# The last group's attention by row tiles, and form steps placed anew, in a two-layer hybrid decoder trunk

## The chip, the cores and the metric

The kernel runs on one core of a Trainium2 chip. The core has a matrix engine (TensorE, here PE, whose weight loads are shown apart as PEld), a vector engine (VectorE, DVE), a scalar engine (ScalarE, ACT), GpSimd (POOL) and a queue engine (SyncE, SP) that issues transfers; POOL issues transfers too. Each engine works through its own instructions in the order in which they were written and stops at one whose inputs are not ready. The metric is the device time of one execution in microseconds (us), lower is better.

## The reference

`x` has 256 rows and 2048 columns, all in float32. Two layers of this, and a last RMSNorm:

```python
h = rms_norm(x, norm_g)
p = split_columns(einsum("bsd,de->bse", h, w_in))     # fox, diff, moba, gla: q, k, v, g each
fox  = forgetting_attention(...)        * silu(p["fox_g"])
diff = rms_norm(differential_attention(...)) * silu(p["diff_g"])
moba = moba_attention(...)              * silu(p["moba_g"])   # 256 rows: one causal block
gla  = rms_norm(gla_chunked(...))       * silu(p["gla_g"])
mixed = concatenate([fox, diff, moba, gla], axis=-1)  # 4 groups of 512 columns, 4 heads each
x = x + einsum("bse,ed->bsd", mixed, w_out)
```

In `moba_attention` 256 rows are one key block, so it is causal softmax attention `softmax(q k^T / sqrt(128)) v` for four heads. With two row tiles of 128 rows, row tile 0 attends to keys 0 to 127 alone, row tile 1 to both halves of the keys.

## The kernel before

**Weights.** Every weight step loads 128x1024 numbers (a `raw` tile; `RAW_BUFS` of them) and splits them into two parts of reduced precision, `hi` (ACT) and `lo` (DVE, `raw` minus `hi`); four pairs of part tiles exist (`PART_BUFS`). The activations are split in the same way: `hTh`/`hTl` for the input projection (`hTp` in the rows), `mTh`/`mTl` for the output projection. PE then makes three products, hi x hi, hi x lo and lo x hi, for each k tile and both row tiles: 12 matmuls of 128x512 for a step. Some projections are formed in pairs from sums and differences of two weight matrices ("form steps", in the rows those with `raw<-xs,raw` or `xs<-xs,raw` on DVE); the table `FORMS_AT` says after which projection step of a layer each of them stands.

**Order.** The program is written out by a planner in Python. The list of PE's weight steps (`plan`) is fixed; between its matmuls, `fill` lets helper tasks (the four groups' attention) put in their instructions when a cost model says that their inputs are ready (`passive` for PE and the queues, `choose` for ACT and DVE). `STALL`, `LOADED`, `ISSUE` and the like are constants of this model. What comes out is one fixed order for each engine. All recorded operations carry the line of the helper, L481 (in the changed kernel L482).

**The end of a layer.** The output projection has four blocks of 512 columns: c0, c1, c2 and chunk 3. The groups are multiplied in the order gla, fox, diff and last moba (`OUT_ORDER`), two steps for each group and block. `moba`'s `attend` makes the scores, the softmax and a transposition; the transposed weights go out to memory (`far<-four`, SP) and come back (`four<-far`, POOL) for each row tile. Then 12 P·V matmuls of 128x128 (4 for row tile 0, 8 for row tile 1) write a PSUM tile `side<-four,four`, DVE multiplies by the gate (`four<-side,four`), and `split_group` makes `mTh` on ACT and `mTl` on DVE, in two halves by heads (`PIECES`). `attend` waits for the transposed weights of both row tiles before its first P·V matmul. The first output block's last two steps need the halves ("m", l, 4) and ("m", l, 5); c2's steps for the third group (`side<-hi,mTh` and the like) stand right before them on PE.

**Gated linear attention.** For each of two pairs of heads DVE makes factors for 7 levels. In the wide way (`GLA_WIDE`), 7 multiplications write one tile of 128 partitions (`four<-eight,four`), and two ACT copies spread it over the zero-padded tile `tq`; in the other way 14 multiplications of 64 partitions write `tq` at once (`tq<-eight,four`). Layer 0 uses the wide way, layer 1 the other. `tq` is a weight of PE's `side<-tq,eight`.

## Time and profile before

| | |
|---|---|
| median of 3 runs | 884.09 us (883.62 to 884.95) |
| the profiled execution | 883.46 us |
| its span, first to last instruction | 881.7 us |
| busy: PE, PEld | 865.9 us (98%), 734.0 us (83%) |
| busy: DVE, ACT, POOL | 763.5 us (87%), 600.7 us (68%), 61.1 us (7%) |
| TensorE's granted clock, mean | 0.998 of full speed |
| moved by DMA | 235.99 MB, 268 GB/s on average |

The profiled execution's time is the span and 1.8 us around it. Busy shares are averages over the span; where one engine waits for another is read from the waits and the timeline of the stretch in question. A wait is put down to the producer that came last by the profile.

### The profile page before, as it was taken

How to read it: one execution, taken by the hardware profiler on the slowest of the kernel's cores; microseconds unless marked ns; L12 is line 12 of the kernel's file. 1: busy time of each engine (PE TensorE's matmuls, PEld its weight loads, DVE VectorE, ACT ScalarE, POOL GpSimd, SP SyncE). 2: the span in 40 equal slices, each digit the busy share in tenths (PEclk: the TensorE clock that was granted, in tenths of full speed). 3: DMA queues.
4: the chain of work that ended last, by engine and by line, in shares of the span. 5: the costliest groups of instructions: out<-in, count | busy, mean ns of one | idle time of the engine just before them, and what ended most of it. 6: DMA issues, size and time to landing. Idle time of an engine off the chain costs nothing.

```text
span 881.7 us, 12530 instructions
## 1 busy us (share of the span) xinstructions
PE 865.9 (98%) x4276; PEld 734.0 (83%) x4276; DVE 763.5 (87%) x993; ACT 600.7 (68%) x945; POOL 61.1 (7%) x82
## 2 busy tenths in 40 slices
PE   9999999999999999999999999999999999999996
PEld 7998788798878888887899888888888788888786
DVE  5779999999999989766768799999999999987583
ACT  7778966756787586754756985576577776777351
POOL 1000100011001001000000010001110100010000
PEclk9999999999999999999999999999999999999999
DMA  8978958799799968995888896699898999789832
GB/s 299 301 277 290 270 196 262 251 258 319 275 303 293 310 236 259 336 324 191 248 282 299 284 246 245 191 307 259 249 332 286 280 307 310 227 264 338 287 118 96
DMA packets 86264, 235.99 MB, mean 268 GB/s; under 512 B 9768, under 2 KB 30136, under 8 KB 86072
## 3 DMA queue, kind: packets, MB, share of 16 engines
q1 hardware_dynamic: 76936, 202.41, 68.2%
q0 software_dynamic: 8832, 31.99, 14.2%
q10 hardware_dynamic: 432, 0.80, 0.2%
q8 instruction: 33, 0.54, 0.2%
q14 instruction: 31, 0.25, 0.1%
HBM read 212.61 MB, written 22.55 MB: 267 GB/s over the span
## 4 chain that ended last, share of the span: by engine, by line
PE 90%; DVE 3%; DMA 2%; issue 1%; ACT 1%; SPq 0%; POOLq 0%; POOL 0%; DVEq 0%; ACTq 0%
PE mm L481 76%; PE side L481 15%; DVE lo L481 2%; DMA four<-far 1%; DMA xs<-in_weights 1%; DMA raw<-in_weights 1%; DVE four L481 1%; DVE tq L481 0%; DVE raw L481 0%; ACT hi L481 0%; DMA far<-four 0%; DVE eight L481 0%; ACT four L481 0%; DVE xs L481 0%; ACT eight L481 0%
## 5 line engine op out<-in xcount | busy, mean ns | idle before, releaser
L481 ACT ACTIVATE hi<-raw 128x1024 fp32r<-128x1024 f32 (+2 forms) x319 | 317.4, 1009 | 151.3 <-PE mm L481 76.5
L481 DVE TENSOR_TENSOR lo<-raw,hi 128x1024 fp32r<-128x1024 f32 (+2 forms) x319 | 362.8, 1156 | 53.4 <-ACT hi L481 46.0
L481 PE MATMUL mm<-hi,hTp 128*128 128x512 f32 (+1 forms) x1440 | 353.5, 379 | 1.1 <-ACT hTp L481 0.4
L481 PEld LDWEIGHTS mm<-hi,hTp 128*128 128x128 f32 x1440 | 262.7, 188 | 50.8 <-issue 1.9
L481 PE MATMUL mm<-lo,hTp 128*128 128x512 f32 (+1 forms) x720 | 196.4, 378 | 0.2 <-DVE lo L481 0.2
L481 PEld LDWEIGHTS mm<-lo,hTp 128*128 128x128 f32 x720 | 131.8, 188 | 25.5 <-DVE lo L481 2.1
L481 PE MATMUL mm<-hi,mTh 128*128 128x512 f32 (+1 forms) x384 | 110.4, 385 | 5.4 <-ACT mTh L481 3.0
L481 PE MATMUL mm<-lo,mTh 128*128 128x512 f32 (+1 forms) x384 | 108.7, 381 | 0.7 <-DVE lo L481 0.7
L481 PE MATMUL mm<-hi,mTl 128*128 128x512 f32 (+1 forms) x384 | 108.6, 381 | 0.0
L481 ACT ACTIVATE hi<-xs 128x1024 fp32r<-128x1024 f32 x72 | 76.0, 1061 | 25.2 <-PE mm L481 24.1
L481 DVE TENSOR_TENSOR lo<-xs,hi 128x1024 fp32r<-128x1024 f32 x72 | 86.0, 1217 | 0.9 <-ACT hi L481 0.8
L481 PEld LDWEIGHTS mm<-hi,mTh 128*128 128x128 f32 x384 | 69.0, 188 | 18.6 <-ACT mTh L481 3.4
L481 PEld LDWEIGHTS mm<-lo,mTh 128*128 128x128 f32 x384 | 70.1, 188 | 15.5 <-DVE lo L481 1.8
L481 PEld LDWEIGHTS mm<-hi,mTl 128*128 128x128 f32 x384 | 70.3, 188 | 14.1
L481 DVE TENSOR_TENSOR xs<-xs,raw 128x1024 f32<-128x1024 f32 x48 | 58.4, 1218 | 0.0
L481 POOL DMA_DIRECT2D four<-far x40 | 21.9, 548 | 505.0 <-DVE lo L481 113.9
L481 PEld LDWEIGHTS side<-four,four 128*128 128x128 f32 (+1 forms) x328 | 38.5, 190 | 4.4 <-issue 2.1
L481 PE MATMUL side<-four,four 128*128 128x128 f32 (+3 forms) x328 | 42.0, 293 | 0.1
L481 DVE STREAM_TRANSPOSE four<-four 128x1024 f32<-128x1024 f32 (+1 forms) x34 | 38.3, 1141 | 0.8 <-ACT four L481 0.7
L481 ACT ACTIVATE four<-mm,rstd 128x512 f32<-128x512 f32 (+2 forms) x44 | 28.0, 663 | 15.8 <-PE mm L481 15.4
L481 ACT ACTIVATE four<-side 128x128 f32<-128x128 f32 (+3 forms) x66 | 15.9, 264 | 23.9 <-PE side L481 23.3
L481 ACT ACTIVATE four<-four 128x1024 f32<-128x1024 f32 (+3 forms) x28 | 25.6, 928 | 9.2 <-DMA four<-far 7.8
(142 smaller groups left out, 727.7 us busy)
## 6 DMA issues: line engine op xcount, KB each, us to landing
raw<-in_weights SPq DMA_DIRECT2D x271, 512.0 KB, 5.2
four<-far POOLq DMA_DIRECT2D x34, 512.0 KB, 6.4
far<-four SPq DMA_DIRECT2D x128, 128.0 KB, 3.9
raw<-in_weights SPq DMA_DIRECT2D x46, 348.0 KB, 5.0
xs<-in_weights SPq DMA_DIRECT2D x24, 512.0 KB, 6.0
xs<-in_weights POOLq DMA_DIRECT2D x24, 512.0 KB, 9.2
xs<-in_x SPq DMA_DIRECT2D x4, 512.0 KB, 6.7
kept<-xs SPq DMA_DIRECT2D x1, 2048.0 KB
```

What stands on the lines that cost most here:

```text
L481: op.do()
```

## The change

The last group's attention (moba) of each layer no longer goes through the common end of `attend`: `last_products` takes row tile 0's transposed weights as soon as they are there, makes its 4 P·V matmuls, its gate, `mTh` and `mTl`, and then does the same for row tile 1, whose 8 P·V matmuls may be written up to 1.5 us of model time ahead of their inputs (`safe`). The first output block's two last steps are multiplied by row tiles (`multiply_rows`): first row tile 0 with both steps (12 matmuls), then row tile 1 (12). Beside that, `GLA_WIDE` is set for layer 1 too, there is one raw tile more, three constants of the planner's model are others, and of `FORMS_AT` about a quarter of the entries move by one to four steps. The rows of `MIDDLE` change too, but the projections among them that are steps of their own keep their order in both layers. The number of PE's matmuls is the same.

```diff
-RAW_BUFS = 6
+RAW_BUFS = 7
...
-FORMS_AT = ((26, 29, 31, 32, 33, 33, 33, 34, 35, 35, 35, 35, 36, 36, 37, 37, 38, 38, 39, 39, 40, 40, 40, 41, 43,
+FORMS_AT = ((26, 29, 31, 32, 33, 33, 33, 34, 35, 35, 35, 35, 36, 36, 36, 37, 38, 38, 38, 39, 40, 41, 41, 41, 43,
...
-STALL = 0.3
+STALL = 0.1
...
-LOADED = 6.0
+LOADED = 5.0
...
-ISSUE = 0.45
+ISSUE = 0.6
...
-PIECES = 2
+LAST_STEPS = 0
+LAST_SAFE = -1.5
 GLA_ABS = (True, False)
-GLA_WIDE = (True, False)
+GLA_WIDE = (True, True)
...
-                    if not (op.kind == "do" or op.kind == "t" and due + SAFE <= times.now
+                    if not (op.kind == "do" or op.kind == "t" and due + (SAFE if op.safe is None else op.safe) <= times.now
...
             t0, p0 = yield from joined(boxes[0])
+            if gi == OUT_ORDER[l][-1]:
+                yield from last_products(l, gi, vn, sg, t0, p0, boxes[1], sgt)
+                return
             t1, p1 = yield from joined(boxes[1])
...
+    def last_products(l, gi, vn, sg, t0, p0, box, sgt):
...
+        for h in range(H):
+            matmul(o[:, 0, h], vh[h][0], p0[:, h], True, True)
+        s2.put(t0)
+        yield
+        every = slice(0, H)
+        gate(0, every)
+        yield
+        low = high(0, every)
+        yield
+        low()
+        given_out(("m0", l))
+        t1, p1 = yield from joined(box)
+        for _ in range(LAST_STEPS):
+            yield
+        for h in range(H):
+            matmul(o[:, 1, h], vh[h][0], p1[:, 2 * h], True, False, safe=LAST_SAFE)
+            matmul(o[:, 1, h], vh[h][1], p1[:, 2 * h + 1], False, True, safe=LAST_SAFE)
+        s4.put(t1, vn)
+
+        def results_out():
+            halves = [slice(0, H // 2), slice(H // 2, H)]
+            for hs in halves:
+                gate(1, hs)
+            lows = [high(1, hs) for hs in halves]
...
+            for i, f in enumerate(lows):
+                f()
+                given_out(("m", l, 2 * gi + i))
...
+    def multiply_rows(s, m):
+        b = s["block"]
+        lh, ll = b["lhs"]
+        order = list(enumerate(s["kts"]))
+        products = [(x, part, j, kt) for x, part in ((lh, "hi"), (lh, "lo"), (ll, "hi")) for j, kt in order]
+        for k, (x, part, j, kt) in enumerate(products):
+            matmul(b["ps"][m][:, :b["n"]], x[:, kt, m * P:(m + 1) * P], s[part][:, j], False, s["last"] and k == len(products) - 1, main=True)
...
-        prepare(i + ahead)
+        prepare(i + ahead - (i - 1 in by_rows_at))
...
-            multiply(s)
+            if i in by_rows_at:
+                multiply_rows(s, 0)
+            elif i - 1 in by_rows_at:
+                multiply_rows(s, 0)
+                for z in (plan[i - 1], s):
...
+                    times.now = max([times.now] + [ready[k] for k in z["later"]])
+                    multiply_rows(z, 1)
+            else:
+                multiply(s)
```

**PE, end of layer 0.** In the kernel before, this is the end of block c2 (`side_3516`), the P·V matmuls (`side_3721`, of which one stands further up among the products of c2, not shown) and the start of the first output block (`mm_3261` is row tile 0, `mm_3262` row tile 1):

```order
L481 MATMUL side_3516<-hi,mTl 128x512 x4
L481 MATMUL side_3516<-lo,mTh 128x512 x4
L481 MATMUL side_3721<-four_3629,four_1659 128x128 x2
L481 MATMUL side_3721<-four_3462,four_1659 128x128
L481 MATMUL side_3721<-four_3629,four_1659 128x128 x2
L481 MATMUL side_3721<-four_3462,four_1659 128x128
L481 MATMUL side_3721<-four_3629,four_1659 128x128 x2
L481 MATMUL side_3721<-four_3462,four_1659 128x128
L481 MATMUL side_3721<-four_3629,four_1659 128x128 x2
L481 MATMUL mm_3261<-hi,mTh 128x512
L481 MATMUL mm_3262<-hi,mTh 128x512
L481 MATMUL mm_3261<-hi,mTh 128x512
```

In the changed kernel (c2 is `side_3518`, P·V `side_3633`, the first output block's row tile 0 `mm_3263`):

```order
L482 MATMUL side_3518<-hi,mTh 128x512 x4
L482 MATMUL side_3518<-hi,mTl 128x512 x2
L482 MATMUL side_3633<-four_3632,four_1741 128x128 x8
L482 MATMUL side_3518<-hi,mTl 128x512 x2
L482 MATMUL side_3518<-lo,mTh 128x512 x4
L482 MATMUL mm_3263<-hi,mTh 128x512 x2
L482 MATMUL mm_3263<-lo,mTh 128x512 x2
L482 MATMUL mm_3263<-hi,mTl 128x512 x2
L482 MATMUL mm_3263<-hi,mTh 128x512 x2
L482 MATMUL mm_3263<-lo,mTh 128x512 x2
L482 MATMUL mm_3263<-hi,mTl 128x512 x2
L482 MATMUL mm_3264<-hi,mTh 128x512 x2
```

Row tile 1's 8 P·V matmuls now stand 6 matmuls ahead of c2's end, and 12 products of row tile 0 follow before `mm_3264`, row tile 1, begins; row tile 0's 4 P·V matmuls stand 30 matmuls ahead of these 8. Layer 1's end has the same pattern.

**DVE, layer 0, gated linear attention at about 120 us.** `four1_1081<-mm2_753` takes a projection's results from PSUM, `lo_...` are weight parts, `raw<-xs,raw` sums of a form step, `eight0_997` the factors. Before:

```order
L481 SCALAR_TENSOR_TENSOR four1_1081<-mm2_753,r-1.0_606,four1_1081 128x512
L481 TENSOR_TENSOR eight0_997<-eight0_997,four11_876 128x2x4x16
L481 TENSOR_TENSOR lo_1229<-raw_1110,hi_1228 128x1024
L481 TENSOR_TENSOR lo_1240<-raw_1122,hi_1239 128x1024
L481 TENSOR_TENSOR eight0_997<-eight0_997,four11_876 128x2x8x8
L481 TENSOR_TENSOR lo_1261<-raw_1135,hi_1260 128x1024
L481 TENSOR_TENSOR raw_1159<-xs_83,raw_1159 128x1024
L481 TENSOR_TENSOR raw_1206<-xs_83,raw_1206 128x1024
L481 TENSOR_TENSOR eight0_997<-eight0_997,four11_876 128x2x16x4
```

After, from the same place:

```order
L482 SCALAR_TENSOR_TENSOR four1_1083<-mm2_755,r-1.0_608,four1_1083 128x512
L482 TENSOR_TENSOR eight0_999<-eight0_999,four11_878 128x2x4x16
L482 TENSOR_TENSOR lo_1222<-raw_1101,hi_1221 128x1024
L482 TENSOR_TENSOR lo_1242<-raw_1112,hi_1241 128x1024
L482 TENSOR_TENSOR raw_1124<-xs_83,raw_1124 128x1024
L482 TENSOR_TENSOR raw_1161<-xs_83,raw_1161 128x1024
L482 TENSOR_TENSOR eight0_999<-eight0_999,four11_878 128x2x8x8
L482 TENSOR_TENSOR eight0_999<-eight0_999,four11_878 128x2x16x4
L482 TENSOR_TENSOR lo_1263<-raw_1124,hi_1262 128x1024
```

The two sums and one `eight` operation now stand ahead of the third `lo` (`lo_1263`), which belongs to a form step; before, the third `lo` (`lo_1261`, of a projection step) stood ahead of the sums. On PE, `lo_1263` is used four matmuls after the place where before the projection step of `lo_1261` began; `lo_1261` was used eight matmuls after that place.

**POOL, layer 1, from the reads for gla's second pair to the end of the forgetting attention's keys.** `four5_5816` (before) and `four11_5735` (after) hold transposed keys for the forgetting attention's scores; `rsh` is a reciprocal root for gla's norm:

```order
L481 DMA four0_5315<-far0_5436 128x1024
L1823 DMA xs_83<-in_weights 128x1024 x4
L481 TENSOR_TENSOR rsh_5893<-pw_5892,halfpow_88 128x8
L481 DMA four5_5816<-far1_5826 128x1024
L481 DMA four11_5817<-far2_5829 128x1024
L481 DMA four3_5828<-far3_5883 128x1024
```

After:

```order
L482 DMA four12_5320<-far0_5419 128x1024
L1885 DMA xs_83<-in_weights 128x1024 x4
L482 DMA four11_5735<-far1_5738 128x1024
L482 TENSOR_TENSOR rsh_5860<-pw_5859,halfpow_88 128x8
L482 DMA four7_5785<-far2_5793 128x1024
L482 DMA four10_5786<-far3_5812 128x1024
```

The read of these keys has moved ahead of `rsh`. On ACT the copy that waits for this read has moved too, from behind the three `hi` of the steps ahead of the scores to a place ahead of three `hi`; on PE the scores stand 24 matmuls earlier.

## Rows read from the trace of the kernel before

**Rows 1.** The page's busy time of each engine: microseconds, share of the span, number of instructions.

```profile
PE 865.9 (98%) x4276; PEld 734.0 (83%) x4276; DVE 763.5 (87%) x993; ACT 600.7 (68%) x945; POOL 61.1 (7%) x82
```

**Rows 2.** PE's waits over the whole span: what waited, for which engine's tile, microseconds in total, times, the longest.

```profile
PE mm L481 <- ACT mTh L481: 3.0, 2, 1.5
PE mm L481 <- ACT eight L481: 1.6, 1, 1.6
PE mm L481 <- DVE lo L481: 0.9, 2, 0.7
PE mm L481 <- ACT four L481: 0.8, 1, 0.8
...
PE mm L481 <- DVE four L481: 0.2, 1, 0.2
```

**Rows 3.** Busy time by stretch: the stretch and its length, then for PE, PEld (weight loads), DVE, ACT and POOL the busy time (and instructions), the granted clock, the share of the DMA engines, GB/s.

```profile
112.00:250.00 138.00, 137.83 (x691) 116.51 (x690) 135.13 (x183) 94.77 (x150) 7.88 (x10) 1.00 0.82 263
...
530.00:660.00 130.00, 128.18 (x639) 109.21 (x638) 126.77 (x192) 82.40 (x129) 8.76 (x10) 1.00 0.82 262
```

**Rows 4.** Timeline, end of layer 0: start, duration, engine, operation, what it writes and reads, number of like records, and in brackets idle time before it and what ended it. Each 128x128 f32 matmul leaves two records.

```profile
394.87 1.09 PE L481 MATMUL side<-hi,mTh 128*128 128x512 f32 x4
...
395.80 1.07 PE L481 MATMUL side<-hi,mTl 128*128 128x512 f32 x4
...
397.54 2.53 PEld L481 LDWEIGHTS side<-four,four 128*128 128x128 f32 x22 [0.20 <-DMA four<-far]
397.61 2.65 PE L481 MATMUL side<-four,four 128*128 128x128 f32 x22
...
400.30 1.42 DVE L481 TENSOR_TENSOR four<-side,four 128x256 f32<-128x256 f32 x4 [1.08 <-PE side L481]
...
401.78 1.20 PE L481 MATMUL mm<-hi,mTh 128*128 128x512 f32 x4 [1.51 <-ACT mTh L481]
```

**Rows 5.** Timeline of POOL, end of layer 0: the reads of the two row tiles of the last group's transposed weights are issued.

```profile
382.43 0.55 POOL L481 DMA_DIRECT2D four<-far  x1 [13.88 <-DVE lo L481]
389.85 0.53 POOL L481 DMA_DIRECT2D four<-far  x1 [6.87 <-DMA far<-four]
```

**Rows 6.** DMA issues of two stretches, 383 to 398 us (first row) and 815 to 830 us (the others): queue, number, KB each, microseconds from issue to landing.

```profile
four<-far POOLq DMA_DIRECT2D x1, 512.0 KB, 7.7
...
four<-far POOLq DMA_DIRECT2D x1, 512.0 KB, 5.7
four<-far POOLq DMA_DIRECT2D x1, 256.0 KB, 4.0
```

**Rows 7.** Timeline, end of layer 1: POOL's issue of the read of row tile 1, and PE's weight loads for the P·V products.

```profile
822.16 0.53 POOL L481 DMA_DIRECT2D four<-far  x1 [5.82 <-DMA far<-four]
...
830.23 2.65 PEld L481 LDWEIGHTS side<-four,four 128*128 128x128 f32 x22
```

**Rows 8.** Timeline, layer 1, around the first run of `tq` multiplications.

```profile
537.19 4.19 DVE L481 TENSOR_TENSOR tq<-eight,four 64x128 f32<-64x128 f32 x14
...
545.40 2.01 ACT L481 ACTIVATE hi<-raw 128x1024 fp32r<-128x1024 f32 x2 [6.61 <-DVE raw L481]
...
553.51 0.73 PE L481 MATMUL mm<-lo,mTh 128*128 128x512 f32 x2 [0.72 <-DVE lo L481]
```

**Rows 9.** Timeline, layer 1, five records from 621 to 649 us: behind the second run of `tq` multiplications, and at the scores of the forgetting attention.

```profile
621.49 0.75 DVE L481 SCALAR_TENSOR_TENSOR four<-mm,rstd,four 128x512 f32<-128x512 f32 x1
...
622.39 0.70 PE L481 MATMUL mm<-hi,mTh 128*128 128x512 f32 x2 [0.78 <-ACT four L481]
...
636.88 2.57 POOL L481 TENSOR_TENSOR rsh<-pw,halfpow 128x8 f32<-128x8 f32 x1 [20.68 <-DVE pw L481]
...
647.45 1.06 ACT L481 ACTIVATE four<-four 128x1024 f32<-128x1024 f32 x1 [3.23 <-DMA four<-far]
...
648.56 1.62 PEld L481 LDWEIGHTS side<-four,four 128*128 128x128 f32 x12 [0.39 <-ACT four L481]
```

**Rows 10.** The same step of the gated linear attention in layer 0, where it is done the wide way: DVE's timeline (first two), and ACT's group of copies in the whole kernel (number, busy time, mean ns of one, idle time before them).

```profile
110.04 0.69 DVE L481 TENSOR_TENSOR four<-eight,four 128x128 f32<-128x128 f32 x3
...
111.78 0.89 DVE L481 TENSOR_TENSOR four<-eight,four 128x128 f32<-128x128 f32 x4
...
L481 ACT ACTIVATE tq<-four 64x896 f32<-64x896 f32 x4 | 3.8, 949 | 0.4 <-DVE four L481 0.3
```

**Rows 11.** Timeline, layer 0, around 125 us: DVE (first three) and PE.

```profile
119.98 2.35 DVE L481 TENSOR_TENSOR lo<-raw,hi 128x1024 fp32r<-128x1024 f32 x2
...
123.59 2.36 DVE L481 TENSOR_TENSOR raw<-xs,raw 128x1024 f32<-128x1024 f32 x2
125.86 0.90 DVE L481 TENSOR_TENSOR eight<-eight,four 128x128 f32<-128x128 f32 x4
...
124.36 1.98 PE L481 MATMUL mm<-hi,hTp 128*128 128x512 f32 x8
...
128.14 0.73 PE L481 MATMUL mm<-lo,mTh 128*128 128x512 f32 x2
```

**Rows 12.** The page's costliest groups (two rows: number, busy time, mean ns of one, idle time just before them and what ended most of it) and its DMA issues (last row).

```profile
L481 ACT ACTIVATE hi<-raw 128x1024 fp32r<-128x1024 f32 (+2 forms) x319 | 317.4, 1009 | 151.3 <-PE mm L481 76.5
...
L481 POOL DMA_DIRECT2D four<-far x40 | 21.9, 548 | 505.0 <-DVE lo L481 113.9
...
xs<-in_weights POOLq DMA_DIRECT2D x24, 512.0 KB, 9.2
```

More of the change, by code (lines that the diff above doesn't have):

```diff
@@ L580, in until, with matmul @@
             cur["task"].latest = max(cur["task"].latest, ready[key])
-    def matmul(out, lhsT, rhs, start, stop, tiles=1, main=False, **kw):
+    def matmul(out, lhsT, rhs, start, stop, tiles=1, main=False, safe=None, **kw):
         n = int(np.prod(rhs.shape[1:]))
@@ L1192, in attend @@
         vn, (sgt, sg) = env[name + "_v", l], env[name + "_g", l]
-        split = name in SPLIT_P
+        split = name in SPLIT_P and gi != OUT_ORDER[l][-1]
         if split:
@@ L1219, in attend @@
             yield
+        mixed = yield from s4.take([P, 2 * H, P])
         ops = yield from take_side()
@@ L1243, in attend @@
         yield
-        mixed = yield from s4.take([P, 2 * H, P])
-        pieces = PIECES if gi == OUT_ORDER[l][-1] else 1
-        for i in range(pieces):
-            hs = slice(i * H // pieces, (i + 1) * H // pieces)
-            for m in range(2):
-                at = slice(m * H + hs.start, m * H + hs.stop)
-                v_.tensor_mul(in_squares(mixed.rearrange("p (h m) t -> p m h t", m=2)[:, m, hs]), in_squares(o[:, hs, m]), sg[:, at])
-            if i == pieces - 1:
-                side.put(ops)
-                s4.put(sgt)
-            begin(split_group(l, gi, mixed, "h m", hs), l, gi)
@@ L1585, in hybrid_trunk @@
         plan.append({**z, "block": b, "need": {(b["need"], b["l"], k // (4 if b["need"] == "h" else 2)) for k in z["kts"]}})
+    by_rows_at = set()
+    for i, s in enumerate(plan[:-1]):
+        z = s.get("block")
+        if z and s["kts"][0] // 4 == OUT_ORDER[z["l"]][-1] and z["need"] == "m" and z is blocks[z["l"] * LAYER + LAYER - 4] and not s["last"]:
+            assert plan[i + 1].get("block") is z and plan[i + 1]["last"]
+            by_rows_at.add(i)
+            for t in plan[i:i + 2]:
+                t["later"], t["need"] = t["need"], {("m0", z["l"])}
     xts = []
@@ L2133, in hybrid_trunk @@
                     b["banks"], b["ps"] = zip(*[take_bank() for _ in range(2)])
-            multiply(s)
+            if i in by_rows_at:
[3 more added lines that the diff above has]
+                for z in (plan[i - 1], s):
+                    loads["left"] = lasts(s)
+                    fill()
+                    while not z["later"] <= ready.keys():
+                        tick(False)
+                    times.now = max([times.now] + [ready[k] for k in z["later"]])
+                    multiply_rows(z, 1)
+            else:
+                multiply(s)
             if s["last"] and b["done"]:
```

36 lines of the change are left out of this document (30 added, 6 removed).

## The prediction, made before the changed kernel ran

> **What bounds the kernel now.** I read the busy shares first: PE is busy 98% of the span and DVE 87% [rows 1]. So a gain can only come out of the little time in which PE stands still, and that is the second view, PE's waits: 6.5 us in the five kinds shown [rows 2], the rest, under 2 us, at the very start. The reader is to see there which waits the change can reach. The largest, 3.0 us for ACT's `mTh`, is two waits of 1.5 us, one at the end of each layer. The 1.6 us for ACT's `eight` falls at 100 us, where the order of all engines is the same in both kernels, so it stays. DVE `lo`, ACT `four` and DVE `four` add 1.9 us. The third view, busy time by stretch, tells what stands behind the smaller waits: in 112 to 250 us DVE works 135.13 of 138 us, in 530 to 660 us 126.77 of 130 [rows 3]. In these two stretches, where each layer's gated linear attention runs, DVE is nearly as full as PE, and one more DVE microsecond in front of a weight part is paid by PE. The last view is the timeline around each of the named waits.
>
> **Last group, layer 0.** PE's last c2 products lead to 11 P·V matmuls (22 records, 397.61 to 400.26); then DVE gates (400.30), ACT makes `mTh`, and PE goes on at 401.78 after 1.51 us of waiting [rows 4]. One matmul takes 0.23 us in the c2 stream (four from 394.87 to 395.80) and 0.24 in P·V (2.65 / 11). The change puts row tile 0's P·V far ahead and row tile 1's behind 18 of c2's 24 matmuls. Behind them stand 6 c2 matmuls and the 12 row-tile-0 products of the first output block: 18 x 0.23 = 4.2 us of cover. The chain that they cover took 400.26 to 401.78 = 1.5 us; with one `lo` (1.2, half of the pair at 119.98 [rows 11]) and one `hi` (1.0 [rows 12]) caught ahead of it in the in-order queues it is 3.7 us, still under 4.2. So the 1.51 us goes. If the cover were gone it would be 1.5 us again.
>
> What is late next is the transfer. Row tile 1's `four<-far` was issued at 389.85 [rows 5] and took 7.7 us to land [rows 6], 397.55; indeed the weight load of P·V already waited 0.20 us for it and began at 397.54 [rows 4], so PE was there at 397.34. Now PE comes with three P·V matmuls more (0.72) and six c2 matmuls fewer (1.39) behind it: 397.34 + 0.72 - 1.39 = 396.67. The wait becomes 0.87, 0.67 more than before. **Layer 0's end: -1.51 + 0.67 = -0.84.** While PE waits there, everything behind it in its queue waits, c2's last products first. Bounds: if the read lands as early relative to PE as in layer 1 there is no wait and the term is -1.7; if it takes 9.2 us like POOL's other 512 KB reads [rows 12], 1.5 later, it is +0.7. I take the row of this transfer itself. Row tile 0's own read (issued 382.43, 4 us like the 256 KB one of layer 1) lands about 386.4; its P·V now comes about 389, so no wait.
>
> **Last group, layer 1.** The same edit, with a quicker read: issued 822.16 [rows 7], landed 5.7 us later [rows 6], 827.9. PE's load there began at 830.23 without a wait [rows 7]; 0.67 earlier is 829.56, still 1.7 us after the landing. **Layer 1's end: -1.5** (bounds 0, if the chain should lose its cover, and -1.6).
>
> **GLA_WIDE in layer 1.** It takes away 2 x 14 DVE multiplications `tq<-eight,four` (one run of 14 took 4.19 us [rows 8]) and sets 2 x 7 `four<-eight,four` in their place; layer 0, which has them already, shows 0.69 us for 3 and 0.89 for 4, 1.58 together [rows 10]. DVE saves 2.6 us a pair. ACT gets four copies of 0.95 us [rows 10]; it stood idle for 6.61 us just there (ended 545.40 [rows 8]), and DVE's 7 plus two copies end 3.5 us after their start, before the 4.19 of now. So the copies cost nothing; without that idle time they would be 3.8 us. What is freed: PE's wait of 0.72 for `lo` at 553.51 [rows 8], 16 us behind the first run; then 0.78 at 622.39 [rows 9], put down to ACT, while DVE's `four<-mm,rstd` ended only at 621.49 + 0.75 = 622.24 and is the real last one; and 0.2 for DVE `four` [rows 2]. All lie behind a run and each is under 2.6 us: **-1.7**. Bounds: 0, if the moved form steps bring as much work forward as was saved, and -2.4 with the 0.39 us that a weight load lost at 648.56 [rows 9] and what the planner's moves may win besides.
>
> **FORMS_AT, layer 0.** Nothing is saved on DVE here, but a form step's matmuls move before the projection step at 124 us, and two sums `raw<-xs,raw` move with them ahead of its `lo` on DVE. From the rows of now [rows 11]: two `lo` from 119.98 to 122.3, the two sums 2.3 (123.59 to 125.86), two `eight` 0.4 (0.90 for 4), then the `lo` 1.2: done at 126.2. PE wants it four matmuls after 124.36, at 125.28: a wait of 0.9 which is not there now. The present one (0.2 for `lo` at 128.14, the second of the two in [rows 2]) goes, since PE then comes later to it. As DVE is full in this stretch, small waits after it shrink too. I take **+0.5**, bounds -0.3 and +0.9.
>
> **At nothing:** the seventh raw buffer and the other planner constants. No raw transfer is in PE's waits [rows 2], and ACT's idle time ahead of `hi<-raw` ended mostly with PE freeing a part buffer (76.5 of 151.3 us [rows 12]), of which there are four as before. The cover is the loads in flight; were it gone, a read of 512 KB, 5.7 us in [rows 6], would be on the path. The re-cut gates and splits of the last group are the same elements in some more or fewer instructions, inside the covered chain.
>
> **The sum:** -0.84 - 1.5 - 1.7 + 0.5 = -3.5 us. The profiled execution took 883.46 us, so 879.9; it lies 0.6 below the median of the runs, 884.09, so I predict **880.6** for the median. All bounds together: -1.7 - 1.6 - 2.4 - 0.3 = -6.0 (878.1) and +0.7 + 0 + 0 + 0.9 = +1.6 (885.7).
>
> **Rivals.** (1) *DVE stays the bound.* The relief in layer 1 is eaten by form steps moved forward, and layer 0 pays the full 0.9: -0.84 - 1.5 + 0 + 0.9 = -1.4, 882.7. For it: two stretches with DVE at 97 to 98% [rows 3]. Against: 5.2 us less DVE work in layer 1.
> (2) *The wait moves to the transfer.* Row tile 1's read lands later than now, by as much as one DVE instruction of 1.2 us (if POOL has to stand back for DVE while it writes the read): layer 0's end becomes +0.4, the sum -2.3, 881.8. Against it: POOL's 40 issues took 548 ns on average beside a DVE that was busy 87% of the time [rows 1, 12], and the three of the last groups shown 0.53 to 0.55 [rows 5, 7]. The Trainium skill ("SBUF — State Buffer", section "SBUF: two separate sides") says that descriptors of a transfer from the GpSimd queue can't be written while DVE runs a two-port operation such as an fp32 copy. By that rule the issue would stretch to the end of the DVE instruction; these issue times show no such stretching.
> (3) *Slower: the fox scores of layer 1.* PE's score rows, which now wait 0.39 us at 648.56 for a transposed tile [rows 9], move up by 24 matmuls (4.9 us), and on ACT the copy that waits for this tile's `four<-far`, now idle 3.23 us for it at 647.45 [rows 9], comes to stand ahead of three `hi`, which PE needs directly behind the scores. If the read landed no earlier than now, PE would stop for 4.9 us: -3.5 + 4.9 = +1.4, 885.5; if it also took 9.2 us where this one took 8 or less, 6.1: +2.6, 886.7. Against the change it decides once the read lands less than 1.4 us earlier than now. Against this rival: the transposition on DVE moves up with PE's rows, and past two `lo` as well, and its issue on POOL, which came behind the `rsh` operation (2.57 us, [rows 9]), now stands ahead of it.
> (4) *No change at the ends*: the planner's split is undone by later waits for the same parts, so only the DVE terms stay: -1.2, 882.9.
>
> **Chances.** Forecast (faster by 2.2 to 6 us) 0.61; rival 1 0.12, rival 2 0.10, rival 3 0.10, rival 4 0.07. A measurement of this kernel can tell about 0.2%, 1.8 us, from no change: below 882.3 is faster. Forecast and rival 2 lie there; rivals 1 and 4 within; rival 3 ends slower by more than that with 0.08 of its 0.10. Faster 0.71, same 0.21, slower 0.08. The likeliest case's own range is 878.6 to 882.2. For 8 in 10 I take 878.4 (nearly all gains at their best) to 883.4, which holds rivals 1, 2 and 4 and leaves out the slower one.
>
> **What would show it.** Right: no wait for `mTh` at the ends of the layers; about 0.9 us for DMA `four<-far` in front of P·V in layer 0 and none in layer 1; a wait for DVE `lo` of up to 0.9 us near 125 us; DVE's busy time lower by some 5 us and ACT's up by 4; hardly a wait between 530 and 660 us. Wrong: a new wait of over 1 us for ACT `hi` or `four` at the fox scores of layer 1, a P·V wait of over 1.5 us, or DVE waits between 530 and 660 us that are as long as now.

## The result and the profile after

The changed kernel takes **876.24 us** (median of 6 runs, 875.97 to 876.48) where the kernel before took 883.50 beside it (882.77 to 884.95): ratio **0.9916 [0.9904, 0.9929]**, 7.3 us faster. The forecast was 880.6 with a range of 878.4 to 883.4: the direction was right, the gain twice as large as expected and outside the range. Three executions that took far longer than the rest (1767.89 us in e6, 1461.56 in e10, 1085.96 of the kernel before beside e11 and e12) are left out of every time given here.

The page of the kernel after, busy time of each engine (order as in [rows 1]):

```profile
PE 864.1 (99%) x4276; PEld 735.0 (84%) x4276; DVE 757.3 (87%) x979; ACT 603.6 (69%) x951; POOL 59.5 (7%) x82
```

PE's waits in the kernel after (as [rows 2]):

```profile
PE mm L482 <- ACT eight L482: 1.6, 1, 1.6
PE side L688 <- PEq L2247: 0.8, 1, 0.8
PE mm L482 <- DVE lo L482: 0.3, 1, 0.3
PE mm L482 <- DVE hTp L482: 0.2, 1, 0.2
PE mm L482 <- ACT hi L482: 0.2, 1, 0.2
```

The two waits for `mTh`, 3.0 us before, are gone, and so are those for ACT `four` and DVE `four`. The span fell from 881.7 to 874.7 us, the granted clock stayed at 0.997 (0.998 before). The same two stretches as in [rows 3], kernel after:

```profile
112.00:250.00 138.00, 137.53 (x692) 117.13 (x691) 135.25 (x181) 95.38 (x150) 7.89 (x10) 1.00 0.81 264
530.00:660.00 130.00, 130.00 (x652) 111.68 (x650) 124.56 (x180) 87.58 (x135) 8.78 (x10) 1.00 0.81 263
```

In 530 to 660 us PE no longer stands still at all, and it gets 652 matmuls done where it did 639. In 112 to 250 us nothing has moved much.

**Where the 7.0 us lie.** Every kernel here has 4276 matmul records, so the start of the n-th record can be compared between traces (up to each of the records in the heading they hold the same number of matmuls of each shape, but for 4 of them at 810 us in e10 and e2). Below, for every kernel that ran: how much each stretch of records became longer or shorter against the trace of before, in us. The heading gives the record that ends the stretch and when it starts in the kernel before.

```
record               100    900   1800   2000   2600   3200   3700   3900   4100   sum
before, us            22    188    374    418    540    662    767    810    853
after              -0.46  -0.21  +0.04  -1.81  +0.00  -2.94  -0.08  +0.00  -1.55  -7.00
e1_old_ends        -0.18  -0.23  -0.01  -0.05  +0.00  -2.95  -0.08  +0.00  +0.01  -3.48
e4_split_alone     -0.55  -0.03  +0.09  -1.81  +0.00  -0.23  -0.03  +0.00  -1.55  -4.12
e7_pv_early        -0.52  -0.23  -0.01  -0.71  +0.00  -2.92  -0.08  +0.00  -1.57  -6.04
e8_pv_late         -0.14  -0.21  +0.01  -1.81  +0.00  -2.91  -0.08  +0.00  -1.75  -6.90
e5_wide_alone      -0.40  -0.01  +0.01  -0.05  +0.00  -1.47  -0.18  +0.00  +0.05  -2.04
e9_wide_and_forms  -0.63  -0.16  +1.32  -0.05  +0.00  -2.94  +0.50  +0.00  +0.05  -1.92
e10_forms_alone    -0.56  -0.25  +1.32  -0.03  +0.00  +7.64  +1.65  +0.51  +2.81 +13.08
e2_narrow_gla      -0.57  -0.24  -0.01  -1.81  +0.00  +5.39  +3.70  +1.13  -1.05  +6.55
e3_six_raws        -0.20  -0.21  +0.47  -1.81  +0.00  -2.91  -0.09  +0.00  -1.75  -6.50
e11_split_and_wide -0.54  -0.03  +0.21  -1.81  +0.00  -1.04  -0.18  +0.00  -1.33  -4.72
e6_old_forms       -0.46  -0.01  +0.00  -1.81  +0.00  -1.38  +7.63  +0.00  -1.75  +2.22
e12_split_wide_7   -0.41  +0.03  +0.01  -1.81  +0.00  -1.38  +3.92  +0.00  -1.75  -1.38
```

The first column is not put down to the change: every other trace starts earlier than the one of before, by 0.14 to 0.63 us, whatever was changed. What the change does stands in four columns: layer 0 up to 188 us (-0.2), the end of layer 0 (-1.8), layer 1's gated linear attention (-2.9) and the end of layer 1 (-1.55).

**The ends.** Timeline of the kernel after, end of layer 0 (answers to [rows 4, 5]): POOL's issue of row tile 1's read, PE's P·V loads, the gate, `mTh`, and PE's first output product of row tile 0; below, the DMA view of 382 to 397 us (as [rows 6]).

```profile
388.77 0.53 POOL L482 DMA_DIRECT2D four<-far  x1 [6.53 <-DMA far<-four]
...
396.06 1.98 PEld L482 LDWEIGHTS side<-four,four 128*128 128x128 f32 x16
...
398.27 0.76 DVE L482 TENSOR_TENSOR four<-side,four 128x256 f32<-128x256 f32 x2 [4.41 <-PE side L482]
...
398.73 0.75 ACT L482 ACTIVATE mTh<-four 128x256 fp32r<-128x256 f32 x2 [6.13 <-DVE four L482]
...
399.46 0.62 PE L482 MATMUL mm<-hi,mTh 128*128 128x512 f32 x2
```

```profile
four<-far POOLq DMA_DIRECT2D x1, 512.0 KB, 5.8
```

The read landed at 388.77 + 5.8 = 394.6, 1.5 us before PE came for it, so the P·V loads carry no wait. `mTh` is done at 399.5, while PE is busy with c2's rest and then with row tile 0 until 402. At the end of layer 1 (as [rows 7]) one small wait is left, for row tile 0's read; the read of row tile 1, in the second row, is in time for the loads of the third:

```profile
816.68 0.97 PEld L482 LDWEIGHTS side<-four,four 128*128 128x128 f32 x8 [0.38 <-DMA four<-far]
...
817.41 0.53 POOL L482 DMA_DIRECT2D four<-far  x1 [5.33 <-DMA far<-four]
...
824.29 1.98 PEld L482 LDWEIGHTS side<-four,four 128*128 128x128 f32 x16
```

**Gated linear attention.** The wide way in layer 1 (as [rows 8, 10]): 1.50 us on DVE for a pair where 4.19 stood, and two ACT copies beside it:

```profile
534.75 1.50 DVE L482 TENSOR_TENSOR four<-eight,four 128x128 f32<-128x128 f32 x7
...
536.29 1.92 ACT L482 ACTIVATE tq<-four 64x896 f32<-64x896 f32 x2
```

The place near 125 us (as [rows 11]), kernel after:

```profile
123.46 0.61 PE L482 MATMUL mm<-lo,mTh 128*128 128x512 f32 x2
...
124.26 0.74 PE L482 MATMUL mm<-hi,mTh 128*128 128x512 f32 x2 [0.18 <-ACT hi L482]
124.48 1.22 DVE L482 TENSOR_TENSOR lo<-raw,hi 128x1024 fp32r<-128x1024 f32 x1
124.84 0.63 PE L482 MATMUL mm<-hi,mTl 128*128 128x512 f32 x2
...
125.76 0.73 PE L482 MATMUL mm<-lo,mTh 128*128 128x512 f32 x2 [0.29 <-DVE lo L482]
...
126.33 1.53 PE L482 MATMUL mm<-hi,hTp 128*128 128x512 f32 x6
```

The pair at 123.46 stands 0.455 us behind the one before it (123.01), as in any full stretch. From it to 126.33 there are four such steps, 1.82 us, and they took 2.87: the place costs 1.05 us where 0.9 was forecast, 0.6 of it at the wait for `lo` and the rest at one for ACT's `hi`, which the forecast did not have. But the stretch up to 188 us ends 0.2 us ahead.

**Fox scores of layer 1** (as [rows 9]): the copy comes without a wait for its read, and PE's scores without a wait for the copy.

```profile
634.60 1.11 ACT L482 ACTIVATE four<-four 128x1024 f32<-128x1024 f32 x1
...
638.99 2.53 PEld L482 LDWEIGHTS side<-four,four 128*128 128x128 f32 x16
```

### The profile page after: what moved, and what is told of

Read it like the earlier page. It is cut to its first block, busy times and chain, and to the rows that moved or that the text cites. A ratio compares the mean times of both kernels' runs of the same rounds, so it can differ in the third digit from the quotient of the medians.

```text
span 874.7 us, 12524 instructions
## 1 busy us (share of the span) xinstructions
PE 864.1 (99%) x4276; PEld 735.0 (84%) x4276; DVE 757.3 (87%) x979; ACT 603.6 (69%) x951; POOL 59.5 (7%) x82
## 4 chain that ended last, share of the span: by engine, by line
PE 97%; DVE 1%; issue 1%; DMA 0%; SPq 0%; ACT 0%; POOLq 0%; POOL 0%; DVEq 0%
PE mm L482 82%; PE side L482 15%; DMA raw<-in_weights 0%; DVE lo L482 0%; DVE raw L482 0%; DVE four L482 0%; ACT eight L482 0%; SPq L1665 0%; DVE eight L482 0%; SPq L1718 0%; POOLq L2254 0%; POOL rf L482 0%; ACT hi L482 0%; DVE xs L482 0%; DVEq L2254 0%
## 5 line engine op out<-in xcount | busy, mean ns | idle before, releaser
L482 ACT ACTIVATE mTh<-four 128x1024 fp32r<-128x1024 f32 (+2 forms) x20 | 17.5, 886 | 19.4 <-DVE four L482 17.6
```

The costliest lines, as they stand in the source:

```text
L482: op.do()
```

## The experiments

### The ends of the layers

**e1_old_ends.** The changed kernel with the common end of `attend` and whole output steps put back.

```diff
-            if gi == OUT_ORDER[l][-1]:
-                yield from last_products(l, gi, vn, sg, t0, p0, boxes[1], sgt)
-                return
...
-            if i in by_rows_at:
-                multiply_rows(s, 0)
...
+            multiply(s)
```

> The changed kernel with the last group's end as it was before: common end of attend, both row tiles' P·V together, gates and splits in two halves by heads, first output block multiplied with both row tiles at a time. GLA_WIDE, FORMS_AT, MIDDLE and the seventh raw tile stay as changed. Theory A (the split is worth what PE slipped at the two ends, 1.8 us each by start times, and no wait took its place): 876.2 + 3.4 to 3.6 = 879.6 to 879.8, with two waits for ACT mTh of 1.5 us back. Theory B (the ends were worth only the 2.3 us of the prediction and the rest of the gain has another source): 878.5.

Measured: 879.95 us (879.64 to 880.14), ratio 0.9959 [0.9947, 0.9972], 3.7 above the changed kernel. The timeline shows both waits again, with the same 1.51 us as in [rows 4]:

```profile
401.32 1.19 PE L481 MATMUL mm<-hi,mTh 128*128 128x512 f32 x4 [1.51 <-ACT mTh L481]
...
831.09 1.19 PE L481 MATMUL mm<-hi,mTh 128*128 128x512 f32 x4 [1.51 <-ACT mTh L481]
```

In the table only the two columns of the ends change. The split is worth 3.3 us in the trace (1.76 + 1.56), 3.7 in the medians.

**e4_split_alone.** The other side: the kernel before with the split, and all tables, the gated linear attention and six raw tiles as they were.

```diff
+            if gi == OUT_ORDER[l][-1]:
+                yield from last_products(l, gi, vn, sg, t0, p0, boxes[1], sgt)
+                return
...
+            if i in by_rows_at:
+                multiply_rows(s, 0)
```

> The kernel before with nothing changed but the last group by row tiles and the first output block multiplied by row tiles; GLA_WIDE, FORMS_AT, MIDDLE, six raw tiles and the constants are those of before. Theory A: both ends give what they gave in the changed kernel, 3.4 to 3.6 us less than before, 880.0. Theory B (as predicted: in layer 0 the read lands 7.7 us after its issue and P·V waits 0.9 us): 2.4 to 2.8 us less, with a wait for DMA four<-far ahead of P·V in layer 0.

Measured: 879.56 us (879.37 to 881.12), ratio 0.9959 [0.9946, 0.9971], 4.0 faster than before. The same -1.81 and -1.55. In its end of layer 0 the read takes longer than in the kernel after: issued at 388.95, it lands 6.6 us later, at 395.55, and there is still no wait:

```profile
388.95 0.53 POOL L482 DMA_DIRECT2D four<-far  x1 [5.37 <-DMA far<-four]
...
396.20 1.98 PEld L482 LDWEIGHTS side<-four,four 128*128 128x128 f32 x16
```

The split stands by itself; it needs none of the other parts. With the forecast's 7.7 us the read would have landed at 396.65, 0.45 us behind the load at 396.20; no trace with the split holds such a landing, the longest is 7.2 us (e11), also without a wait.

**e7_pv_early.** Does the read of row tile 1 become the wait if P·V comes earlier? P·V stands 12 matmuls further ahead.

```diff
-LAST_SAFE = -1.5
+LAST_SAFE = -5.0
```

> The changed kernel with LAST_SAFE -5 instead of -1.5: row tile 1's P·V stands 12 matmuls of c2 (2.7 us) earlier on PE; beside it one lo on DVE moves. It asks when the read of row tile 1 lands. Theory A (it lands 5.4 to 6.6 us after its issue, as in the runs so far): PE, 1.5 us behind the landing in layer 0 and 2.3 in layer 1, now waits 0.4 to 2.0 us in layer 0 and about 0.4 in layer 1, and nothing of that comes back: 876.2 + 0.8 to 2.4 = 877.0 to 878.6. Theory B (7.7 us as in the one trace of before is its usual time): a wait of 3 us in layer 0, 879.2 or more.

Measured: 877.88 us (877.45 to 879.30), ratio 0.9938 [0.9927, 0.9950], 1.6 above the changed kernel. Timeline, end of layer 0:

```profile
389.34 0.53 POOL L482 DMA_DIRECT2D four<-far  x1 [7.41 <-DMA far<-four]
...
394.46 2.02 PE L482 MATMUL side<-four,four 128*128 128x128 f32 x16 [0.87 <-DMA four<-far]
```

The read landed 5.0 us after its issue, at 394.34, and PE waited 0.87 for it (1.1 us in the table). So a wait moves to the transfer when P·V is put this far ahead. It is not rival 2 itself, in which the read lands later: here it landed sooner than in the kernel after.

**e8_pv_late.** How much cover does the chain behind P·V need? P·V stands behind all of c2 and six products of row tile 0.

```diff
-LAST_SAFE = -1.5
+LAST_SAFE = 0.5
```

> The changed kernel with LAST_SAFE +0.5: row tile 1's P·V stands behind c2 and behind the first six row-tile-0 products, so only six products (1.4 us) cover gate and mTh of row tile 1 instead of 18 matmuls (4.1 us). Theory A (the chain needs 1.5 us, and a lo or hi ahead of it in the queues up to 2.2 more): PE waits 0.2 to 1 us at each layer's end, 876.6 to 878.2. Theory B (the chain of one half is shorter than the cover left): no wait, 876.2.

Measured: 876.45 us (876.10 to 876.62), ratio 0.9917 [0.9904, 0.9930]: as the changed kernel. Timeline, end of layer 0:

```profile
399.29 1.95 PE L482 MATMUL side<-four,four 128*128 128x128 f32 x16
...
401.73 0.75 ACT L482 ACTIVATE mTh<-four 128x256 fp32r<-128x256 f32 x2 [6.12 <-DVE four L482]
...
402.46 0.62 PE L482 MATMUL mm<-hi,mTh 128*128 128x512 f32 x2
```

P·V is over at 401.24; `mTh` is done at 402.48, 1.24 us later; six matmuls (1.4 us) cover it and PE, which needs only the first half of it at 402.46, does not wait. Of the forecast's 4.2 us of cover, two thirds were not needed here: nothing stood ahead of the chain on DVE or ACT.

### The wide way and the table

**e5_wide_alone.** The kernel before with the wide way in layer 1.

```diff
-GLA_WIDE = (True, False)
+GLA_WIDE = (True, True)
```

> The kernel before with GLA_WIDE on in layer 1 and nothing else changed (the form steps stay by the old table; the planner moves some PE steps around the two runs by itself). Theory A (the DVE work saved is what frees PE in layer 1, with or without the moved form steps): PE slipped 3.0 us by start times between 550 and 660 us, so 883.6 - 2.5 to 3.0 = 880.6 to 881.1. Theory B (it takes the moved form steps as well; alone the relief only shifts the wait): less than 1 us off, 882.6 or more.

Measured: 881.90 us (881.34 to 882.50, 11 runs), ratio 0.9980 [0.9971, 0.9988], 1.7 faster: the forecast's price for this part. The table has -1.47 up to 662 us. PE's only wait in 530 to 660 us:

```profile
PE mm L481 <- DVE lo L481: 1.1, 1, 1.1
```

Order and read of the end of layer 0 are those of before, and here the read took 5.4 us to land and P·V began without a wait. The 7.7 us of [rows 6] are the longest landing of this read in the 14 traces; the shortest is 5.0 us (e7).

**e9_wide_and_forms.** The same and the new `FORMS_AT`; six raw tiles, old ends.

```diff
-FORMS_AT = ((26, 29, 31, 32, 33, 33, 33, 34, 35, 35, 35, 35, 36, 36, 37, 37, 38, 38, 39, 39, 40, 40, 40, 41, 43,
+FORMS_AT = ((26, 29, 31, 32, 33, 33, 33, 34, 35, 35, 35, 35, 36, 36, 36, 37, 38, 38, 38, 39, 40, 41, 41, 41, 43,
...
-GLA_WIDE = (True, False)
+GLA_WIDE = (True, True)
```

> The kernel before with GLA_WIDE on in layer 1 and the new FORMS_AT; six raw tiles and the old ends. PE's, and POOL's order is that of e1 (which has seven raw tiles). Theory A (the parts add up: wide 1.7, table 1.2, seventh tile 0.7): 883.6 - 2.9 = 880.7, that is 0.7 over e1. Theory B (the table gives nothing by itself and the seventh tile is what the rest of e1's gain came from): as e5, 881.9.

Measured: 880.53 us (880.17 to 882.55), ratio 0.9971 [0.9960, 0.9982]. In 530 to 660 us PE is busy without a gap, as in the changed kernel (columns as in [rows 3]), and the stretch is 2.94 us shorter:

```profile
530.00:660.00 130.00, 130.00 (x652) 111.81 (x651) 124.53 (x180) 86.81 (x134) 8.92 (x11) 1.00 0.83 270
```

So the second half of that gain, 1.47 us, is the table's beside the wide way. But between 188 and 374 us this kernel loses 1.3 us that the changed kernel does not, and 0.5 more up to 767 us: in the traces it ends where e5 does (-1.92 and -2.04), and the intervals of the two overlap.

**e10_forms_alone.** The kernel before with the new table alone.

```diff
-FORMS_AT = ((26, 29, 31, 32, 33, 33, 33, 34, 35, 35, 35, 35, 36, 36, 37, 37, 38, 38, 39, 39, 40, 40, 40, 41, 43,
+FORMS_AT = ((26, 29, 31, 32, 33, 33, 33, 34, 35, 35, 35, 35, 36, 36, 36, 37, 38, 38, 38, 39, 40, 41, 41, 41, 43,
```

> The kernel before with the new FORMS_AT alone; the narrow way in layer 1, six raw tiles, old ends. Theory A (the table was set for the wide way and moves form steps to where DVE now has room; in the narrow way it piles DVE work up, as e2 showed with +14 us): 3 to 14 us slower than before, 887 to 898. Theory B (the table is better by itself and e2's loss came from the new ends or the seventh tile): 882.5 or less.

Measured: 896.95 us (896.57 to 897.52), ratio 1.0153 [1.0139, 1.0166], **13.4 slower**. PE's waits, whole span (the first stands at the end of layer 1, at 843.41, most of the others between 620 and 656 us):

```profile
PE side L481 <- DMA four<-far: 3.1, 1, 3.1
...
PE mm L481 <- DVE lo L481: 2.6, 5, 0.7
PE mm L481 <- DVE four L481: 2.5, 2, 2.1
PE mm L481 <- ACT hi L481: 2.3, 3, 1.9
```

**e2_narrow_gla.** The changed kernel with the narrow way in layer 1.

```diff
-GLA_WIDE = (True, True)
+GLA_WIDE = (True, False)
```

> The changed kernel with GLA_WIDE off in layer 1: 14 multiplications of 64 partitions for each pair of heads instead of 7 and two ACT copies; form steps as changed. Theory A (the DVE work saved in layer 1 is what freed PE's 3.0 us between 530 and 660 us): slower by 2.5 to 3.5 us, 878.7 to 879.7, with waits for DVE back in that stretch. Theory B (the moved form steps did it, or did most of it): slower by under 1 us.

Measured: 890.28 us (889.78 to 891.15), ratio 1.0078 [1.0065, 1.0090], 14 above the changed kernel. PE's waits in 530 to 660 us:

```profile
PE mm L482 <- ACT hi L482: 1.9, 1, 1.9
PE mm L482 <- DVE four L482: 1.6, 1, 1.6
PE mm L482 <- DVE lo L482: 1.5, 3, 0.7
```

Both kernels with the new table and the narrow way fail in the same stretch (+5.4 and +7.6). The planner writes much of layer 1 in another order then, so neither run gives the price of 14 multiplications; they show that the new table goes with the wide way only: 896.95 and 883.6 us with the narrow way (new table, old table), 880.5 and 881.9 with the wide one.

A part of the loss is the clock. In both traces PE stops for 1.9 us for ACT `hi` (at 649.80 in e2, 653.49 in e10), and behind that TensorE's granted clock, 1.00 before, is 0.57 of full speed in 651 to 655 us (e2) and 0.51 in 654 to 661 us (e10), the lower of its two levels (1.2 and 2.4 GHz) for most of the time. 128x512 matmuls start 0.43 us apart there instead of 0.23, an estimated 1.6 us more in e2 (8 matmuls, 0.2 us each) and 3 in e10 (15). A stop of 3.1 us in e10 (at 843.41) was not followed by such a fall. The stretch of e10 (columns as in [rows 3], the clock is the third from the end):

```profile
654.00:661.00 7.00, 6.44 (x17) 4.49 (x16) 7.00 (x7) 6.10 (x8) 0.00 (x0) 0.51 1.00 375
```

### The seventh raw tile

**e3_six_raws.** The changed kernel with six raw tiles. The order of PE, DVE and POOL is the same.

```diff
-RAW_BUFS = 7
+RAW_BUFS = 6
```

> The changed kernel with six raw tiles. PE's, DVE's and POOL's order stay the same, ACT's but for two instructions, SP's transfers stand a little elsewhere. Theory A (the seventh tile does nothing for the time): 876.2, within 0.5 us, and the read of row tile 1 in layer 0 still lands before PE wants it. Theory B (the seventh tile spreads the weight loads and so made that read land in 5.8 us instead of 7.7): P·V of layer 0 waits 0.7 to 0.9 us for it, 877.0, and the start of the kernel is 0.4 us longer, 877.4.

Measured: 876.96 us (876.25 to 877.16), ratio 0.9924 [0.9910, 0.9937], 0.7 above the changed kernel; the intervals overlap, so the medians alone do not show it, and the trace tells more. ACT's waits for raw transfers, in the kernel before, the changed kernel and this one:

```profile
ACT hi L481 <- DMA raw<-in_weights: 17.0, 13, 2.3
```

```profile
ACT hi L482 <- DMA raw<-in_weights: 7.0, 7, 1.7
```

```profile
ACT hi L482 <- DMA raw<-in_weights: 14.1, 13, 2.8
```

Timeline near 287 us, first this kernel, then the changed one:

```profile
286.89 1.06 ACT L482 ACTIVATE hi<-raw 128x1024 fp32r<-128x1024 f32 x1 [0.90 <-DMA raw<-in_weights]
```

```profile
287.52 1.06 ACT L482 ACTIVATE hi<-raw 128x1024 fp32r<-128x1024 f32 x1 [1.21 <-PE mm L482]
```

With six tiles `hi` waits for its weights, with seven for PE to free a part tile. The stretch up to 374 us is 0.47 us longer, with a PE wait for DVE's `lo` in it (0.16 shown, at 301.93) that the changed kernel has not. In e9 and e10, also six tiles and the new table, it is +1.32; there a wait for DVE `four` (0.42 shown in e9) comes first, whose way back to the raw transfers was not followed. With the old table and six tiles that stretch shows at most +0.2: the tile is wanted by the new table.

### The table and the tile together

**e6_old_forms.** The changed kernel with the old `FORMS_AT`.

```diff
-FORMS_AT = ((26, 29, 31, 32, 33, 33, 33, 34, 35, 35, 35, 35, 36, 36, 36, 37, 38, 38, 38, 39, 40, 41, 41, 41, 43,
+FORMS_AT = ((26, 29, 31, 32, 33, 33, 33, 34, 35, 35, 35, 35, 36, 36, 37, 37, 38, 38, 39, 39, 40, 40, 40, 41, 43,
```

> The changed kernel with the old FORMS_AT. Theory A: GLA_WIDE and the split carry the gain; the new table is worth 0.5 us at most: 875.9 to 876.9, the wait near 125 us in layer 0 that the new table brought is gone and the old small ones are back. Theory B (the table is needed for the relief in layer 1): 1.5 to 3 us slower, 877.7 to 879.2, with DVE waits between 530 and 660 us.

Measured: 884.20 us (880.37 to 888.66), ratio 1.0013 [0.9997, 1.0029], 8.0 above the changed kernel; in the trace 7.6 us are lost between 662 and 767 us. Timeline there, and below it the stretch of 754 to 757 us (columns as in [rows 3]):

```profile
743.97 0.53 POOL L482 DMA_DIRECT2D four<-far  x1 [0.94 <-ACT hi L482]
...
750.08 1.06 ACT L482 ACTIVATE four<-four 128x1024 f32<-128x1024 f32 x1 [2.89 <-DMA four<-far]
...
751.04 3.88 ACT L482 ACTIVATE hi<-raw 128x1024 fp32r<-128x1024 f32 x4
...
752.13 0.73 PE L482 MATMUL mm<-hi,mTh 128*128 128x512 f32 x2 [2.25 <-ACT hi L482]
```

```profile
754.00:757.00 3.00, 3.00 (x15) 2.90 (x15) 3.00 (x5) 1.87 (x2) 0.00 (x0) 0.50 0.73 228
```

This is rival 3 in another attention: a copy that waits for a fetched tile stands on ACT ahead of four `hi`, and PE needs the first of them. Behind the stop TensorE's granted clock is 0.50 (1.2 GHz), and 128x128 matmuls start 0.21 us apart instead of 0.12. The stop and the clock are the 3.7 us by which this trace loses more than the one of e12 (below), where neither is seen. The other 3.9 go to waits for DVE `four` (1.1 shown, at 727.29), ACT `hi` (0.3) and DVE `lo` (0.7), none of which the changed kernel has there.

**e11_split_and_wide.** Is the old table itself at fault? The kernel before with the split and the wide way, old table, six raw tiles.

```diff
+            if gi == OUT_ORDER[l][-1]:
+                yield from last_products(l, gi, vn, sg, t0, p0, boxes[1], sgt)
+                return
...
-GLA_WIDE = (True, False)
+GLA_WIDE = (True, True)
```

> The kernel before with the two parts of the change that name a mechanism: the last group's end by row tiles and the wide way in layer 1; the old FORMS_AT, the old planner constants, six raw tiles. Why this run: going back to the old table in the changed kernel cost 8.7 us, 7.75 of them between 727 and 771 us, but it left the new planner constants in place, and with the old table these constants do change the order (70 PE rows, all in layer 1); with the new table they change nothing. Theory A (the old table alone is not harmful, the loss belonged to the old table together with the new constants): the parts add up, -1.8 at the end of layer 0, -1.5 in 530 to 660 us, -1.55 at the end of layer 1, no stop of PE between 727 and 771 us: about 4.8 us under the kernel before, 878.5 to 879. Theory B (the new table is needed as soon as the split and the wide way come together): the 7.75 us are there again, some 886, with ACT's copy of the fetched tile ahead of four hi as in the run with the old table.

Measured: 878.49 us (878.15 to 878.90), ratio 0.9947 [0.9931, 0.9962], 4.8 faster than before; no loss between 662 and 767 us. Theory A's number, though not all its parts: -1.04 up to 662 us, with a PE wait of 1.1 for ACT `hi` left, and -1.33 at the end of layer 1. On ACT no copy of a fetched tile waits for its read between 715 and 762 us:

```profile
741.01 2.00 ACT L482 ACTIVATE four<-four 128x1024 f32<-128x1024 f32 x2
```

**e12_split_wide_seven.** The same with seven raw tiles.

```diff
-RAW_BUFS = 6
+RAW_BUFS = 7
```

> The same with a seventh raw tile; the order of every engine is that of the run with six. Against the changed kernel only FORMS_AT is then another (the planner constants change nothing beside the new table), so the difference to it is what the new table is worth. Theory A (the seventh tile matters only with the new table, as the stage from 267 to 374 us was no slower than before in runs with the old table and six tiles): within 0.3 us of the run with six tiles, and the table worth about 1.5 to 2 us, all of it in 530 to 660 us. Theory B (the seventh tile is worth 0.6 us with any table): 0.6 under the run with six.

Measured: 883.19 us (881.78 to 886.77), ratio 1.0007 [0.9992, 1.0021]: **4.7 slower than with six**. Neither theory. A premise in both expectations was wrong: beside the old table it is the seventh tile that changes the order (70 rows of PE), and with seven tiles the constants change nothing. So e12 has the order of e6 on every engine, and the difference between the two is none of the program's. Its timeline at the same place:

```profile
743.17 0.53 POOL L482 DMA_DIRECT2D four<-far  x1 [0.82 <-ACT hi L482]
...
748.05 1.06 ACT L482 ACTIVATE four<-four 128x1024 f32<-128x1024 f32 x1 [0.89 <-DMA four<-far]
...
750.17 0.30 PEld L482 LDWEIGHTS mm<-hi,mTh 128*128 128x128 f32 x2 [0.40 <-ACT hi L482]
```

From the issue to the copy that waits for it went 6.1 us in e6 and 4.9 here. The other waits are much like e6's, but at the place of its long stop PE hardly waits, and the granted clock in 754 to 757 us is 1.00. With one order, the stretch cost 7.6 us in the one trace and 3.9 in the other, and the times of the two kernels spread over 8 and 5 us, where those of the others spread over 0.5 to 2.4. That the landings make this spread, by the stop and the clock behind it, fits the two traces and the mean clocks of the executions: 0.998 in the shortest of e6 (880.37 us) and 0.992 in the longest, 0.998 and 0.996 in e12. Over more than two traces it is not shown.

Table and tile by medians, all with the split and the wide way: old table 878.5 with six tiles and 883.2 or 884.2 with seven; new table 877.0 with six and 876.2 with seven. Together they are worth 2.3 us, the table alone 1.5, the tile alone less than nothing. That the tile costs time beside the old table is shown for the order that the planner writes then, not for the tile as such.

**The planner's three constants** set back in the changed kernel, and the old `MIDDLE` in it, give the same order on every engine: no edits at all, beside this table and tile.

## Why the prediction was wrong in size

The mechanisms were mostly as described; terms of the sum were mis-sized. Of the 4.4 us between forecast and measurement, 1.2 lie in layer 1's stretch (-1.7 forecast, -2.94 measured, beyond the bound of -2.4), 1.0 at the end of layer 0, 0.7 in `FORMS_AT` of layer 0 and 0.5 in the start of the traces. Some 0.9 more lie in the step from the profiled execution to the median: the forecast added 0.6 because the median of 3 runs, 884.09, lay that far above it; over 6 runs it was 883.50, level with the profiled 883.46, and after the change the median lies 0.2 below the profiled 876.48.

**The end of layer 0, -0.84 forecast, -1.81 measured: a term that failed.** The wait was found and removed as described, but the forecast put 0.67 us of new waiting for the read against it, since it took the one landing of [rows 6], 7.7 us, as the price. The same read took 5.4 us in e5, whose order there is that of before, and 5.0 (e7), 5.4 (e1), 5.8 (after), 6.6 (e4) and 7.2 (e11) elsewhere. It is also issued earlier against PE than the forecast's sum has it: 7.3 us ahead of the P·V load in the trace after (388.77 and 396.06), 6.8 in the forecast (389.85 and 396.67), so that even 7.7 us would have cost 0.4 and not 0.87. The bound "no wait, -1.7" was the right case. A second, smaller part: the idle time shown, 1.51 us, is less than the 1.76 that PE lost by starts (after against e1), since the shown end of the matmul before it lies behind the moment at which the next could have begun. Two like pairs of matmuls start 0.455 us apart and are shown 0.62 long, which is 0.16 of that; the rest is not taken apart. The Trainium skill ("Perfetto Trace Analysis", section "Tensor Engine Instruction (MATMUL, LD_WEIGHTS)") says that the profile's end of a matmul is an estimate from its size. The trace agrees: these pairs are shown to overlap by 0.16 us.

**The end of layer 1, -1.5 forecast, -1.55 measured: right.** No wait for row tile 1's read. It would be -1.75 (e8, e12) without the 0.38 us on row tile 0's read, which the forecast did not look at.

**Layer 1's stretch, -1.7 forecast, -2.94 measured: the term that failed most.** The three waits of before are gone, as said, and DVE's busy time in the changed kernel is 6.2 us lower and ACT's 2.9 higher, about as said. Two things failed. The waits were priced at the idle time shown, 1.7 us together; with no wait left (after, e9) the stretch is 2.94 us shorter by starts, and the weight load's 0.39 us of [rows 9], which the forecast left to the bound, is only a part of the difference. And the forecast priced `FORMS_AT` only in layer 0; layer 1's moves stood in the bounds alone, "what the planner's moves may win besides". With the wide way alone (e5) the three waits are gone too, but a new one of 1.1 us for DVE `lo` comes, at 648.12; the new places take it away, and e9 shows that they do. That e5 came out at -1.7 in the medians and -1.47 in the trace, near the forecast, is luck: a price too low and a wait not foreseen cancel.

**`FORMS_AT` in layer 0, +0.5 forecast, -0.2 measured.** The loss came where it was said, near 125 us, and 1.05 us large where 0.9 was said; for `lo` it is 0.6 of that, so the size is in part luck. That it would still be there at the end of the stretch was wrong: seven of the eight kernels with the new table (after, e1, e2, e3, e7, e8, e10) are 0.20 to 0.25 us *ahead* at 188 us, and e9 0.16; the five with the old one are within 0.03. The waits of before behind that place are gone, among them one for `lo` at 165.28 (0.17 shown); that PE came later to them and met the work of DVE done fits, but was not shown by a run.

**The seventh raw tile, "at nothing".** The forecast looked for raw transfers in PE's waits, found none, and stopped. ACT's waits show them: 17.0 us in 13 waits before, 7.0 in 7 after. Beside the new table it is worth 0.4 us in the stretch up to 374 us (e3) and 0.7 in the medians, which is not clear of the noise; with the old table, where it changes the planner's order, it costs 4.7 (e12 against e11).

**The rivals.** 1 and 4 did not come. 2 did not come: the read landed sooner, not later, and the issues on POOL took 550 ns on average (x40), as before. 3 did not come at the fox scores, since the read was in time (no wait at 634.60), but its mechanism, with the clock behind it, is 3.7 us of e6's loss; in e12 it costs next to nothing. By stretches: -0.2 - 1.8 - 2.9 - 1.55 = -6.5, and 0.46 is the start of the traces.

**What stays open.** Why e10 and e2 lose so much more than the 2 x 2.6 us of DVE work that the narrow way adds is open but for the part of the clock: the order of layer 1 differs too widely. Nor was it tried which of the table's entries bring the 1.47 us.

## What to carry to other kernels

Price a transfer by all landings of its kind that the traces hold, and give the range; one landing is a draw. A copy that waits for it, placed ahead of work that PE needs, can cost its delay and then the clock (e6); moving such a copy alone was not tried. An edit that is "at nothing" in the waits of the bound engine should be looked up once more in the waits of the engines that feed it. Where a planner writes the order, tables, buffer counts and algorithmic switches are one setting: the new table is 13.4 us slower alone, the seventh tile 4.7 us slower beside the old table, and together with the wide way they give some 3.7 us (e1), so part-by-part prices do not add. The edit with its own stretch adds better: at the end of layer 0 the split gives -1.81 in every kernel that has it as chosen, at the end of layer 1 between -1.05 and -1.75.

## What was not expected of the hardware

The landing of one and the same 512 KB read, issued at the same place of the same order, took 5.4 us in one trace and 7.7 in another (e5, before), at a second place 4.9 and 6.1 (e12, e6). Stretches whose order did not change repeat to within 0.05 us over 120 us between traces (the column that ends at 540 us), so this spread does not reach the time everywhere: it does where an engine waits for a transfer. Where such a wait made PE stop for 2.25 us (e6), the granted clock was 0.50 afterwards, in 754 to 757 us, and the clock added to the loss; stops of 1.9 us for ACT `hi` were followed by the same in e2 and e10, and one of 3.1 us in e10 was not.
